# A streaming encoder step on one core: own values in one full-shape product, spatial products joined, one unread product more at the start, the last norm by logarithm and exponential

## The chip, the cores and the metric

The kernel runs on one core of a Trainium2 chip. The metric is the device time of one execution in microseconds (us); lower is better. TensorE multiplies (PE, with its weight loads in a queue called PEld), VectorE (DVE), ScalarE (ACT) and GpSimd (POOL) work on tiles of 128 partitions, and transfers are issued from the queues of SP, ACT and POOL.

## The reference

Two layers and a final norm run over 256 prompt rows and 8 x 16 sample rows, 384 rows in all, with a model width of 2048. Layer 0 is two kinds of attention side by side; layer 1 is a gated MLP with a spatial mix. Cut to the parts that the change touches:

```python
# layer 0, samples: cached and new keys and values are joined, per head
go = fox_core(gq, k_all, v_all, ...)      # softmax weights @ (128 cached + 16 new) values
to = sb_core(tq, sk_all, sv_all, ...)     # stick-breaking weights @ the same
# layer 1: 16 groups of 256 columns, one lower-triangular 128x128 matrix each
w = jnp.where(causal, w_sp[:, :L, :L], 0.0)
mixed = jnp.einsum('gts,bnsgc->bntgc', w, vg) + b_sp   # prompt: 128-row chunks; samples: 16 rows each
h = h + einsum('bsn,nd->bsd', u * mixed * silu(z), w_out1)
# the end
y = h * rsqrt(mean(h * h, -1) + 1e-6) * final_g
```

## The kernel before

All 384 rows are one batch of three blocks of 128 rows (tb = 0 and 1 the prompt, tb = 2 the eight samples). The large products keep fp32 precision by splitting both operands into a high and a low part: `products` (lines 100 to 102) issues three products of 128x512 for each block of rows and each 128 rows of a weight matrix. The weights come by SP (`wload`), ACT makes the high part (line 84), DVE the low part (line 86). Everything else is fitted in between these dense products.

The order on each engine is fixed when the program is built: the framework puts ready instructions into the queues by a model of their times, so a step can stand far ahead of the code next to it. An engine then takes its queue strictly in that order.

**Attention.** Heads are worked in 8 pairs (`quad` has four heads, `attended` finishes a pair). In `head`, the samples' weights against the 16 new keys of each sample stand as a 128x32 block, which DVE turns in 32x32 blocks into `own` (line 718). The samples' output `od` is summed in PSUM from four 32x32 products with `own` (line 728), one for each group of two samples, and eight products with the cached values (line 732; 128 rows by 32 columns of the array). The prompt's output is three full 128x128 products (lines 734 to 736). These products are in plain fp32, and the trace shows each as two records. PT, the turned weights that lines 732 to 736 need, come back from DRAM through POOL's queue and a DVE transpose (line 721).

**Spatial mix.** For each of eight chunks c of 512 columns, three blocks tb and two groups i, lines 932 to 934 issue three products of 256 columns into half a PSUM bank, and line 937 adds the bias and multiplies by the gate.

**Start.** `keep_warm` issues products of ones that nobody reads. The first block of x is turned on TensorE (line 248), three transposes, the third of rows that another transfer brings.

**End.** `last` makes the last four of 32 weight blocks for each block of rows in five pieces; DVE adds the piece to h1 (line 994), ACT sums squares (line 996), DVE multiplies by the gain (line 998). `norm` then has DVE prepare the mean (lines 1002 to 1004), POOL take the power -0.5 (line 1005), and ACT and DVE scale the rows (lines 1012, 1015) and send them out. `norm(0)` and `norm(1)` stand ahead of the last block's pieces, `norm(2)` ends the program.

Of the kernel before, what the change touches and what calls it, by code (L numbers as in the profile page):

```python
# [8 lines left out]
F32 = mybir.dt.float32  # L9
F32R = mybir.dt.float32r  # L10
AF = mybir.ActivationFunctionType
# [4 lines left out]
P = 128  # L16
# [21 lines left out]
def tile_hybrid_step(  # L38
# [20 lines left out]
    def nm(s):  # L59
        n_names[0] += 1  # L60
        return f"{s}_{n_names[0]}"
# [100 lines left out]
    with ExitStack() as l0:  # L162
# [76 lines left out]
        def x_blocks(k):  # L239
            b = lp.tile([P, 2 * T], F32, tag="PT", name=nm("xT"))  # L240
            then("DVE", lambda: V.transpose(out=b, in_=xblk[k]))
            xblk[k], xblk[k + 1] = b[:, :T], b[:, T:]

        def x_transposes(k):
            if k < FB:
                b = bank()
                for tb in range(NT):
                    then("PE", lambda: PE.transpose(b[:, tb * P:(tb + 1) * P], xs[k // 4][:, tb, k % 4 * P:k % 4 * P + P], ident))
            else:
                b = xblk[k]  # L250
# [89 lines left out]
        with late():  # L340
            V.tensor_reduce(out=par[:, 4:5], in_=par[:, :4], axis=AX.X, op=ALU.add)
            V.tensor_scalar(out=slotb[:, 0:1], in0=par[:, 4:5], scalar1=-1.0, scalar2=-NEG, op0=ALU.add, op1=ALU.mult)
            V.tensor_scalar(out=slotb[:, 1:2], in0=par[:, 4:5], scalar1=NEG, scalar2=None, op0=ALU.mult)
        masks = []
        for strict in (0, 1):
# [6 lines left out]
            for s in range(2):  # L352
                with late():
                    V.tensor_scalar(out=md[:, s * P:(s + 1) * P], in0=md[:, s * P:(s + 1) * P], scalar1=slotb[:, s:s + 1], scalar2=None, op0=ALU.add)
            new = lp.tile([P, 2 * T], F32, tag="PT", name=nm("new"))[:, :P]
            V.memset(new, 0.0)
# [29 lines left out]
        def forget(o):  # L386
# [39 lines left out]
            gains(1)  # L426
            nFT = lp.tile([8, 2 * T], F32, tag="PT", name="nFT")[:, :T]
            V.tensor_scalar(out=nFT, in0=FT, scalar1=-1.0, scalar2=None, op0=ALU.mult)
# [219 lines left out]
        def head(g, h, kT, values, qT, kc, vc, gate):  # L648
            fox = g < 2
            mp, md = masks[0 if fox else 1]  # L650
            if fox:

                fb = lp.tile([P, 2, T], F32, tag="fb", name=nm("fb"))
                fc = lp.tile([P, P], F32, tag="fc", bufs=1, name=nm("fc"))
                G.dma_start(fb[:, 0, :2 * P], nFd[h, :2 * P].partition_broadcast(P))
                G.dma_start(fb[:, 0, 2 * P:], nFd[h, :P].partition_broadcast(P))
                G.dma_start(fb[:, 1, 2 * P:TW], nFd[h, 2 * P:].rearrange("(j k) -> j k", k=32).unsqueeze(1).broadcast_to([4, 32, 32]))
                G.dma_start(fc, nFcd[:, h, :].unsqueeze(1).broadcast_to([8, 16, P]))
                G.tensor_tensor(out=fb[:, 0, :], in0=fb[:, 0, :], in1=mp, op=ALU.add)
                G.tensor_tensor(out=fb[:, 1, 2 * P:TW], in0=fb[:, 1, 2 * P:TW], in1=md[:, 2 * P:], op=ALU.add)  # L660
                G.tensor_tensor(out=fb[:, 1, :2 * P].rearrange("p (s k) -> p s k", s=2), in0=md[:, :2 * P].rearrange("p (s k) -> p s k", s=2),
                                in1=fc.unsqueeze(1).broadcast_to([P, 2, P]), op=ALU.add)
                mp, md = fb[:, 0, :], fb[:, 1, :TW]

# [51 lines left out]

            own = lp.tile([P, 32], F32, tag="own", bufs=4, name=nm("own"))
            V.transpose(out=own, in_=weights[:, 5 * P:])
            blk = yield
            PT = lp.tile([P, 2 * T], F32, tag="PT", name=nm("PT"))[:, :5 * P]  # L720
            yield V.transpose(out=PT, in_=blk)
# [3 lines left out]
            od, ot = ob[:, 2 * P:3 * P], ob[:, :2 * P]  # L725
            for j in range(4):
                js = slice(32 * j, 32 * j + 32)
                PE.matmul(od[js, :], lhsT=own[js, :], rhs=vn[js, 2, :], start=True, stop=False)
            for s in range(2):
                for j in range(4):  # L730
                    js = slice(32 * j, 32 * j + 32)
                    PE.matmul(od[js, :], lhsT=PD[:, s * P + 32 * j:s * P + 32 * j + 32], rhs=vc[:, 2 * j + s, :], start=False, stop=(s == 1))
            yield
            PE.matmul(ot[:, :P], lhsT=PT[:, 2 * P:T], rhs=vn[:, 0, :], start=True, stop=True)
            PE.matmul(ot[:, P:2 * P], lhsT=PT[:, :P], rhs=vn[:, 0, :], start=True, stop=False)
# [76 lines left out]
    with ExitStack() as l1:  # L812
# [91 lines left out]
        for c in range(8):  # L904
# [10 lines left out]
            else:  # L915
# [7 lines left out]
                for j, ck in enumerate(order[:3]):  # L923
                    aside[ck] = x[:, j, :]
                    G.dma_start(x[:, j, :], wlast(*ck))
            for tb in range(NT):
                m = bank()
                for i in range(2):
                    cs = slice(i * 256, i * 256 + 256)
                    (wh, wl), (vh, vl) = wTs[i], vhl  # L930
                    o = m[:, cs]
                    PE.matmul(o, lhsT=wh[:, tb // 2, :], rhs=vh[:, tb, cs], start=True, stop=False)
                    PE.matmul(o, lhsT=wh[:, tb // 2, :], rhs=vl[:, tb, cs], start=False, stop=False)
                    PE.matmul(o, lhsT=wl[:, tb // 2, :], rhs=vh[:, tb, cs], start=False, stop=True)
                for i in range(2):
                    gh = gate[:, tb, i * 256:(i + 1) * 256]
                    V.scalar_tensor_tensor(out=gh, in0=m[:, i * 256:(i + 1) * 256], scalar=bcol[:, tb // 2, 2 * c + i:2 * c + i + 1], in1=gh, op0=ALU.add, op1=ALU.mult)
            gT = lp.tile([P, NT * 4, P], F32, tag="gTt", bufs=1, name=nm("gTt"))
# [61 lines left out]
        def norm(tb):  # L1000
            r0, r1 = rst2[:, tb, 0:1], rst2[:, tb, 1:2]
            V.tensor_reduce(out=r0, in_=ssq2[:, tb, :4], axis=AX.X, op=ALU.add)
            V.tensor_scalar(out=r0, in0=r0, scalar1=1.0 / DM, scalar2=RMS_EPS, op0=ALU.mult, op1=ALU.add)
            V.scalar_tensor_tensor(out=r0, in0=ssq2[:, tb, 4:5], scalar=1.0 / DM, in1=r0, op0=ALU.mult, op1=ALU.add)  # L1004
            G.tensor_tensor(out=r1, in0=r0, in1=ex[:, 0:1], op=ALU.pow)  # L1005
            ht = h1[3][:, tb, 256:]
# [54 lines left out]
```

## Time and profile before

| | us |
|---|---|
| median of 3 runs (1795.68 to 1795.89) | 1795.76 |
| the profiled execution, its own time | 1797.74 |
| span of the profile | 1796.0 |
| PE busy (share of the span) | 1785.7 (99%) |
| DVE / ACT / POOL busy | 941.9 / 725.3 / 389.5 |

The span covers the first to the last record of the profiled execution, and its own time lies 1.74 us above it. A matmul's duration in a row is longer than its share of the engine, since products overlap in the array: what one costs is the distance between starts in a dense row of them.

### The profile page before, as it was taken

What the parts mean: (1) busy time and instruction counts of PE and PEld (TensorE: products, weight loads), DVE (VectorE), ACT (ScalarE), POOL (GpSimd) and SP (SyncE); (2) the same over time, 40 slices, a digit from 0 to 9 for tenths busy, and PEclk for the clock granted to TensorE, in tenths of its full rate; (3) what the DMA queues carried; (4) which work ended last, traced back from release to release, by engine and by line L of the source; (5) the groups of instructions that cost most, each with busy time, mean ns of one, the idle gap of its engine ahead of it and who ended that gap; (6) DMA issues with size and microseconds to landing.
All of it is one profiled execution on the core that took longest, in us unless ns stands there. A gap on an engine that the chain in (4) does not pass through costs nothing. (4 is left out here: it accounts for less than half of the span.)

```text
span 1796.0 us, 24812 instructions
## 1 busy us (share of the span) xinstructions
PE 1785.7 (99%) x8707; PEld 1477.4 (82%) x8707; DVE 941.9 (52%) x1600; ACT 725.3 (40%) x1301; POOL 389.5 (22%) x584
## 2 busy tenths in 40 slices
PE   9999999999999999999999999999999999999998
PEld 8987788888888788888888888888888888888887
DVE  6337465457448455534434546455555464455366
ACT  5435354346337244433333433433333333433344
POOL 6526543223311211200300121220120210220020
PEclk9999999999999999999999999999999999999999
DMA  7968988768767777644544454455444554455553
GB/s 215 228 187 207 270 219 226 221 176 227 216 188 192 225 199 192 193 136 129 137 129 123 139 159 127 147 148 145 146 147 119 154 154 129 147 144 153 155 146 119
DMA packets 184749, 305.97 MB, mean 170 GB/s; under 512 B 23512, under 2 KB 61968, under 8 KB 184624
## 3 DMA queue, kind: packets, MB, share of 16 engines
q1 hardware_dynamic: 127696, 225.37, 42.9%
q0 software_dynamic: 26096, 62.89, 14.0%
q10 hardware_dynamic: 30832, 16.13, 3.0%
q8 instruction: 68, 1.11, 0.3%
q14 instruction: 57, 0.47, 0.1%
HBM read 268.57 MB, written 29.42 MB: 166 GB/s over the span
## 5 line engine op out<-in xcount | busy, mean ns | idle before, releaser
L86 DVE TENSOR_TENSOR wlo<-raw,whi 128x512 fp32r<-128x512 f32 x784 | 536.7, 693 | 723.8 <-ACT whi L84 722.7
L101 PE MATMUL d<-wlo,slot 128*128 128x512 f32 x2349 | 911.9, 389 | 0.1
L102 PE MATMUL d<-whi,slot 128*128 128x512 f32 x2349 | 911.2, 389 | 0.0
L84 ACT ACTIVATE whi<-raw 128x512 fp32r<-128x512 f32 x784 | 493.2, 631 | 903.0 <-PE d L102 847.2
L100 PE MATMUL d<-whi,slot 128*128 128x512 f32 x2349 | 822.9, 390 | 0.0
L100 PEld LDWEIGHTS d<-whi,slot 128*128 128x128 f32 x2349 | 440.4, 188 | 94.8 <-issue 2.4
L101 PEld LDWEIGHTS d<-wlo,slot 128*128 128x128 f32 x2349 | 441.1, 188 | 91.5 <-DVE wlo L86 1.0
L102 PEld LDWEIGHTS d<-whi,slot 128*128 128x128 f32 x2349 | 441.1, 188 | 90.8
L128 POOL DMA_DIRECT2D gTt<-trn x128 | 77.9, 617 | 312.8 <-issue 159.0
L439 POOL DMA_DIRECT2D slot<-d x48 | 44.0, 923 | 133.3 <-DVE wlo L86 54.3
L884 POOL DMA_DIRECT2D wr<-in_w_sp_dram x64 | 34.9, 552 | 113.0 <-DVE wT L888 99.5
L539 POOL DMA_DIRECT2D slot<-wd x32 | 27.1, 855 | 95.0 <-DMA wd<-pr 39.3
L877 DVE TENSOR_TENSOR slot<-d,slot 128x512 f32<-128x512 f32 x48 | 32.4, 688 | 13.8 <-PE d L102 13.8
L833 POOL DMA_DIRECT2D slot<-in_sgu_ln_g_dram x8 | 4.5, 568 | 135.0 <-PE d L102 135.0
L500 POOL DMA_DIRECT2D kcache<-in_cache_sb_k_dram x32 | 24.9, 785 | 32.1 <-DVE KT L668 32.1
L500 POOL DMA_DIRECT2D kcache<-in_cache_fox_k_dram x32 | 25.0, 788 | 24.8 <-DVE KT L668 23.9
L759 POOL DMA_DIRECT2D blk<-h1d x12 | 10.9, 919 | 72.2 <-DMA h1d<-slot 34.6
L849 POOL DMA_DIRECT2D bcol<-in_b_sp_dram x1 | 1.2, 1176 | 116.1 <-DVE w L848 116.1
L827 POOL TENSOR_SCALAR rsv<-mvr 128x3 f32<-128x3 f32 x1 | 0.5, 538 | 108.1 <-DVE mvr L826 108.1
L824 DVE BATCH_NORM_STATS2 stats<-vt 128x6 f32<-128x512 f32 x24 | 16.2, 689 | 11.6 <-ACT vt L823 11.6
L912 DVE SCALAR_TENSOR_TENSOR gate<-d,rstd,gate 128x512 f32<-128x512 f32 x24 | 17.4, 748 | 7.3 <-PE d L102 7.3
L909 ACT ACTIVATE gate<-d,rstd 128x512 f32<-128x512 f32 x24 | 16.5, 690 | 11.2 <-PE d L102 11.1
(256 smaller groups left out, 1287.5 us busy)
## 6 DMA issues: line engine op xcount, KB each, us to landing
raw<-in_w_in_dram SPq DMA_DIRECT2D x640, 256.0 KB, 2.9
raw<-in_w_out_dram SPq DMA_DIRECT2D x189, 256.0 KB, 3.4
slot<-d POOLq DMA_DIRECT2D x48, 192.0 KB, 6.3
d<-slot ACTq DMA_DIRECT2D x24, 256.0 KB, 4.0
gTt<-trn POOLq DMA_DIRECT2D x128, 48.0 KB, 3.5
wd<-pr ACTq DMA_DIRECT2D x16, 320.0 KB, 5.6
slot<-wd POOLq DMA_DIRECT2D x32, 160.0 KB, 5.1
kcache<-in_cache_fox_k_dram POOLq DMA_DIRECT2D x32, 128.0 KB, 5.5
```

The source lines that it names most:

```text
L84: highs.append(S.activation(hi, raw, AF.Copy).ins)
L86: splits.append(V.tensor_tensor(out=lo, in0=raw, in1=f32(hi), op=ALU.subtract).ins)
L100: PE.matmul(o, lhsT=his[k][:, t], rhs=hi[:, 0, :], start=(k == first), stop=False)
L101: PE.matmul(o, lhsT=his[k][:, t], rhs=lo[:, 0, :], start=False, stop=False)
L102: mm = PE.matmul(o, lhsT=los[k][:, t], rhs=hi[:, 0, :], start=False, stop=(k == last))
L128: G.dma_start(dst[32 * j:32 * j + 32, :, 32 * a:32 * a + 32], trn[32 * a:32 * a + 32, :, 32 * j:32 * j + 32])
L439: r = G.dma_start(blk[32 * j:32 * j + 32].rearrange("p h (a d) -> p (h a) d", d=32), d[:, :, 32 * j:32 * j + 32].rearrange("h (a p) d -> p ...
L500: G.dma_start(k[32 * j:32 * j + 32].rearrange("p (b d) -> p b d", d=32), (c_fox_k, c_sb_k)[n // 8][:, :, n % 8, 32 * j:32 * j + 32].rearra ...
L539: G.dma_start(blk[32 * j:32 * j + 32].rearrange("p j (a d) -> p (j a) d", d=32), wd[:, :, :, 32 * j:32 * j + 32].rearrange("j x (a p) d -> ...
L877: evicted = V.tensor_tensor(out=h1[c][:, tb, :], in0=o[tb], in1=h1[c][:, tb, :], op=ALU.add)
L884: G.dma_start(wr[js, 0, :].rearrange("p (a s) -> p a s", s=32), w_sp[g, :, js].rearrange("(a p) s -> p a s", p=32))
L912: V.scalar_tensor_tensor(out=gate[:, tb, :], in0=o[tb], scalar=rstd[:, tb:tb + 1], in1=gate[:, tb, :], op0=ALU.mult, op1=ALU.mult)
```

## The change

Four edits. (1) `own` is laid out on the diagonal of a 128x128 tile by a POOL multiplication with a mask `diag`, so that the samples' new values take one full product in place of four 32x32 ones, and it is issued behind the cached values instead of ahead of them. (2) The spatial products of a group take both prompt blocks at once (512 columns), the samples' block stays at 256. (3) One unread product of ones stands between the second and third transpose of the first block. (4) `norm` takes the power by ACT: a logarithm, with the mean's last part as scale and bias, and an exponential. Beside these, some tiles change size or tag (`xT` is turned in two halves in other buffers, `PT`, `fb`).

```diff
         def x_blocks(k):
-            b = lp.tile([P, 2 * T], F32, tag="PT", name=nm("xT"))
-            then("DVE", lambda: V.transpose(out=b, in_=xblk[k]))
-            xblk[k], xblk[k + 1] = b[:, :T], b[:, T:]
+            both = xblk[k]
+            for kk in range(2):
+                xblk[k + kk] = b = lp.tile([P, 512], F32, tag="KT", bufs=4, name=nm("xT"))[:, :T]
+                then("DVE", lambda: V.transpose(out=b, in_=both[:, kk * T:kk * T + T]))
...
                 for tb in range(NT):
+                    if k == 0 and tb == 2:
+
+                        keep_warm(1)
                     then("PE", lambda: PE.transpose(b[:, tb * P:(tb + 1) * P], xs[k // 4][:, tb, k % 4 * P:k % 4 * P + P], ident))
...
+        diag = lc.tile([P, 4], F32, name="diag")
+        V.memset(diag, 1.0)
+        select(diag, [[-32, 4]], 0, 1)
+        select(diag, [[32, 4]], 31, -1)
...
-            own = lp.tile([P, 32], F32, tag="own", bufs=4, name=nm("own"))
-            V.transpose(out=own, in_=weights[:, 5 * P:])
+            turned = lp.tile([P, 32], F32, tag="ownT", name=nm("ownT"))
+            V.transpose(out=turned, in_=weights[:, 5 * P:])
+            own = lp.tile([P, P], F32, tag="own", bufs=4, name=nm("own"))
+            G.tensor_tensor(out=own.rearrange("p (j q) -> p j q", j=4), in0=turned.unsqueeze(1).broadcast_to([P, 4, 32]),
+                            in1=diag.unsqueeze(2).broadcast_to([P, 4, 32]), op=ALU.mult)
...
-            for j in range(4):
-                js = slice(32 * j, 32 * j + 32)
-                PE.matmul(od[js, :], lhsT=own[js, :], rhs=vn[js, 2, :], start=True, stop=False)
             for s in range(2):
                 for j in range(4):
                     js = slice(32 * j, 32 * j + 32)
-                    PE.matmul(od[js, :], lhsT=PD[:, s * P + 32 * j:s * P + 32 * j + 32], rhs=vc[:, 2 * j + s, :], start=False, stop=(s == 1))
+                    PE.matmul(od[js, :], lhsT=PD[:, s * P + 32 * j:s * P + 32 * j + 32], rhs=vc[:, 2 * j + s, :], start=(s == 0), stop=False)
             yield
+            PE.matmul(od, lhsT=own, rhs=vn[:, 2, :], start=False, stop=True)
...
-            for tb in range(NT):
-                m = bank()
-                for i in range(2):
-                    cs = slice(i * 256, i * 256 + 256)
-                    (wh, wl), (vh, vl) = wTs[i], vhl
-                    o = m[:, cs]
-                    PE.matmul(o, lhsT=wh[:, tb // 2, :], rhs=vh[:, tb, cs], start=True, stop=False)
...
+            for i in range(2):
+                cs = slice(i * 256, i * 256 + 256)
+                (wh, wl), (vh, vl) = wTs[i], vhl
+
+                for j, tbs in ((0, slice(0, 2)), (1, slice(2, 3))):
+                    n = tbs.stop - tbs.start
+                    m = bank()[:, :n * 256].rearrange("p (t c) -> p t c", t=n)
+                    PE.matmul(m, lhsT=wh[:, j, :], rhs=vh[:, tbs, cs], start=True, stop=False)
...
             V.tensor_scalar(out=r0, in0=r0, scalar1=1.0 / DM, scalar2=RMS_EPS, op0=ALU.mult, op1=ALU.add)
-            V.scalar_tensor_tensor(out=r0, in0=ssq2[:, tb, 4:5], scalar=1.0 / DM, in1=r0, op0=ALU.mult, op1=ALU.add)
-            G.tensor_tensor(out=r1, in0=r0, in1=ex[:, 0:1], op=ALU.pow)
+
+            S.activation(r1, ssq2[:, tb, 4:5], AF.Ln, scale=1.0 / DM, bias=r0)
+            S.activation(r1, r1, AF.Exp, scale=-0.5)
```

How the queues change. TensorE's queue in the second pair of heads, before (a is a PSUM bank of the small products, d one of the dense ones); first where the products with `own` stood, then, 61 rows later, where the rest of the pair stood:

```order
L102 MATMUL d_1752<-whi_2123,slot_136 128x512
L728 MATMUL a_2227<-vnat_647,own_1843 32x128
L100 MATMUL d_2160<-whi_2165,slot_129 128x512
L728 MATMUL a_2227<-vnat_647,own_1843 32x128 x2
L101 MATMUL d_2160<-wlo_2167,slot_129 128x512
L102 MATMUL d_2160<-whi_2165,slot_130 128x512
L100 MATMUL d_2160<-whi_2171,slot_129 128x512
L101 MATMUL d_2160<-wlo_2173,slot_129 128x512
L102 MATMUL d_2160<-whi_2171,slot_130 128x512
L728 MATMUL a_2227<-vnat_647,own_1843 32x128
L100 MATMUL d_2161<-whi_2165,slot_129 128x512
```

```order
L102 MATMUL d_2161<-whi_2314,slot_132 128x512
L732 MATMUL a_2240<-vcache_2083,PT_2223 32x128 x3
L732 MATMUL a_2227<-vcache_2081,PT_2225 32x128 x8
L732 MATMUL a_2240<-vcache_2083,PT_2223 32x128 x5
L734 MATMUL a_2227<-vnat_647,PT_2225 128x128
L735 MATMUL a_2227<-vnat_647,PT_2225 128x128
L736 MATMUL a_2227<-vnat_647,PT_2225 128x128
L734 MATMUL a_2240<-vnat_647,PT_2223 128x128
```

The same pair now, whole:

```order
L102 MATMUL d_2174<-whi_2344,slot_134 128x512
L741 MATMUL a_2239<-vcache_2093,PT_2237 32x128 x8
L741 MATMUL a_2248<-vcache_2095,PT_2235 32x128 x8
L743 MATMUL a_2239<-vnat_657,own_1859 128x128
L744 MATMUL a_2239<-vnat_657,PT_2237 128x128
L745 MATMUL a_2239<-vnat_657,PT_2237 128x128
L746 MATMUL a_2239<-vnat_657,PT_2237 128x128
L743 MATMUL a_2248<-vnat_657,own_1888 128x128
L744 MATMUL a_2248<-vnat_657,PT_2235 128x128
L745 MATMUL a_2248<-vnat_657,PT_2235 128x128
L746 MATMUL a_2248<-vnat_657,PT_2235 128x128
L100 MATMUL d_2174<-whi_2350,slot_133 128x512
```

The products with `own` have left the dense stretch and stand among the full ones. Four of the eight pairs now read like this. In the first pair the cached products of the second head stand behind the first head's full products. In three pairs part of the cached products has moved ahead, as here in the first pair of the third quad:

```order
L741 MATMUL a_4599<-vcache_3426,PT_4597 32x128 x4
L100 MATMUL d_4564<-whi_4567,slot_129 128x512
L101 MATMUL d_4564<-wlo_4569,slot_129 128x512
L102 MATMUL d_4564<-whi_4567,slot_130 128x512
L100 MATMUL d_4564<-whi_4573,slot_129 128x512
L101 MATMUL d_4564<-wlo_4575,slot_129 128x512
L102 MATMUL d_4564<-whi_4573,slot_130 128x512
L741 MATMUL a_4599<-vcache_3426,PT_4597 32x128 x4
L741 MATMUL a_4608<-vcache_3428,PT_4595 32x128 x8
```

ACT's queue at the end of the program, before (sq: the sums of squares of the last block; the slots are h1):

```order
L996 ACTIVATE sq_3237_15974,ssq_15709<-slot_5878 128x256
L996 ACTIVATE sq_3239_15991,ssq_15709<-slot_5878 128x256
L1012 ACTIVATE slot_5875<-slot_5875,rst_15710 128x512
L1012 ACTIVATE slot_5877<-slot_5877,rst_15710 128x256
L1013 DMA out_dram<-slot_5875 128x512
```

and now:

```order
L1006 ACTIVATE sq_3264_15912,ssq_15647<-slot_5884 128x256
L1006 ACTIVATE sq_3266_15929,ssq_15647<-slot_5884 128x256
L1015 ACT_TABLE_LOAD
L1015 ACTIVATE rst_15648<-ssq_15647,rst_15648 128x1
L1016 ACT_TABLE_LOAD
L1016 ACTIVATE rst_15648<-rst_15648 128x1
L1023 ACTIVATE slot_5881<-slot_5881,rst_15648 128x512
L1023 ACTIVATE slot_5883<-slot_5883,rst_15648 128x256
L1024 DMA out_dram<-slot_5881 128x512
```

Two loads of a function table have come in with the logarithm and the exponential; the same four rows stand in `norm(0)` and `norm(1)`, ahead of the last block's squares.

## Rows read from the trace of the kernel before

**Rows 1.** The page, part 1: busy time, share of the span, instructions.

```profile
PE 1785.7 (99%) x8707; PEld 1477.4 (82%) x8707; DVE 941.9 (52%) x1600; ACT 725.3 (40%) x1301; POOL 389.5 (22%) x584
```

**Rows 2.** PE's waits: who, for whom, us in total, times, longest.

```profile
PE a L933 <- DVE vl L91: 0.6, 3, 0.2
```

**Rows 3.** Timeline of PE, first pair: start, us, line, out<-in, records.

```profile
178.09 0.39 PE L102 MATMUL d<-whi,slot 128*128 128x512 f32 x1
178.41 0.42 PE L728 MATMUL a<-vnat,own 32*32 32x128 f32 x8
...
180.59 0.39 PE L735 MATMUL a<-vnat,PT 128*128 128x128 f32 x2
...
181.48 0.39 PE L736 MATMUL a<-vnat,PT 128*128 128x128 f32 x2
...
181.94 0.40 PE L101 MATMUL d<-wlo,slot 128*128 128x512 f32 x1
```

**Rows 4.** Timeline of PE, second pair, whose own products came earlier.

```profile
207.08 0.39 PE L102 MATMUL d<-whi,slot 128*128 128x512 f32 x1
207.40 1.10 PE L732 MATMUL a<-vcache,PT 128*32 128x128 f32 x32
...
210.11 0.39 PE L102 MATMUL d<-whi,slot 128*128 128x512 f32 x1
```

**Rows 5.** Timeline of PE, one own product (two records) among dense ones.

```profile
192.10 0.39 PE L102 MATMUL d<-whi,slot 128*128 128x512 f32 x1
192.42 0.40 PE L728 MATMUL a<-vnat,own 32*32 32x128 f32 x2
...
193.09 0.40 PE L101 MATMUL d<-wlo,slot 128*128 128x512 f32 x1
```

**Rows 6.** The tiles own and fb: ns min/median/max, first and last start.

```profile
L718 DVE STREAM_TRANSPOSE own<-pr x16: 191/197/206, 145.1 to 576.8; 128x32 f32<-128x32 f32 x16
...
L661 POOL TENSOR_TENSOR fb<-md,fc x8: 727/752/1132, 90.9 to 277.7; 128x256 f32<-128x256 f32 x8
```

**Rows 7.** Timeline of PE: nine spatial products in a row; 30 dense ones.

```profile
1001.01 0.28 PE L934 MATMUL a<-vh,wTl 128*128 128x256 f32 x1
...
1001.97 0.28 PE L934 MATMUL a<-vh,wTl 128*128 128x256 f32 x1
...
1777.83 0.39 PE L990 MATMUL d<-wlast,slot 128*128 128x512 f32 x1
...
1784.41 0.39 PE L992 MATMUL d<-wlast,slot 128*128 128x512 f32 x1
```

**Rows 8.** Timeline of ACT at the end; in brackets the idle time ahead.

```profile
1777.27 1.12 ACT L1012 ACTIVATE slot<-slot,rst 128x512 f32<-128x512 f32 x2 [1.00 <-POOL rst L1005]
...
1782.93 0.63 ACT L996 ACTIVATE sq<-slot 128x512 f32<-128x512 f32 x1 [1.42 <-DVE slot L994]
...
1785.62 0.63 ACT L996 ACTIVATE sq<-slot 128x512 f32<-128x512 f32 x1 [1.97 <-DVE slot L994]
...
1788.24 0.42 ACT L996 ACTIVATE sq<-slot 128x256 f32<-128x256 f32 x1 [0.95 <-DVE rst L1003]
1788.57 0.19 ACT L996 ACTIVATION_READ_ACCUMULATOR sq<-slot 128x1 f32 x1
1789.72 1.12 ACT L1012 ACTIVATE slot<-slot,rst 128x512 f32<-128x512 f32 x2 [0.97 <-POOL rst L1005]
```

**Rows 9.** Timeline of ACT around the one table load inside the kernel.

```profile
1014.82 1.28 ACT L909 ACT_TABLE_LOAD   x1
1016.12 0.69 ACT L909 ACTIVATE gate<-d,rstd 128x512 f32<-128x512 f32 x1
```

**Rows 10.** Timeline of PE and its weight loads in the first 11 us.

```profile
5.01 0.18 PEld L248 LDWEIGHTS a<-ident,slot 128*128 128x128 f32 x1 [0.54 <-DMA slot<-in_x_sample_dram]
...
8.21 1.63 PE L282 MATMUL d<-whi,slot 128*128 128x512 f32 x3
9.63 1.07 PE L282 MATMUL d<-wlo,slot 128*128 128x512 f32 x3
```

More of the change, by code (lines that the diff above doesn't have):

```diff
@@ L354, in tile_hybrid_step @@
                     V.tensor_scalar(out=md[:, s * P:(s + 1) * P], in0=md[:, s * P:(s + 1) * P], scalar1=slotb[:, s:s + 1], scalar2=None, op0=ALU.add)
-            new = lp.tile([P, 2 * T], F32, tag="PT", name=nm("new"))[:, :P]
+            new = lp.tile([P, 5 * P], F32, tag="PT", name=nm("new"))[:, :P]
             V.memset(new, 0.0)
@@ L426, in forget @@
             gains(1)
-            nFT = lp.tile([8, 2 * T], F32, tag="PT", name="nFT")[:, :T]
+            nFT = lp.tile([8, 5 * P], F32, tag="PT", name="nFT")[:, :T]
             V.tensor_scalar(out=nFT, in0=FT, scalar1=-1.0, scalar2=None, op0=ALU.mult)
@@ L651, in head @@
             if fox:
-                fb = lp.tile([P, 2, T], F32, tag="fb", name=nm("fb"))
+                fb = lp.tile([P, T + TW], F32, tag="fb", name=nm("fb"))
                 fc = lp.tile([P, P], F32, tag="fc", bufs=1, name=nm("fc"))
-                G.dma_start(fb[:, 0, :2 * P], nFd[h, :2 * P].partition_broadcast(P))
-                G.dma_start(fb[:, 0, 2 * P:], nFd[h, :P].partition_broadcast(P))
-                G.dma_start(fb[:, 1, 2 * P:TW], nFd[h, 2 * P:].rearrange("(j k) -> j k", k=32).unsqueeze(1).broadcast_to([4, 32, 32]))
+                G.dma_start(fb[:, :2 * P], nFd[h, :2 * P].partition_broadcast(P))
+                G.dma_start(fb[:, 2 * P:T], nFd[h, :P].partition_broadcast(P))
+                G.dma_start(fb[:, T + 2 * P:], nFd[h, 2 * P:].rearrange("(j k) -> j k", k=32).unsqueeze(1).broadcast_to([4, 32, 32]))
                 G.dma_start(fc, nFcd[:, h, :].unsqueeze(1).broadcast_to([8, 16, P]))
-                G.tensor_tensor(out=fb[:, 0, :], in0=fb[:, 0, :], in1=mp, op=ALU.add)
-                G.tensor_tensor(out=fb[:, 1, 2 * P:TW], in0=fb[:, 1, 2 * P:TW], in1=md[:, 2 * P:], op=ALU.add)
-                G.tensor_tensor(out=fb[:, 1, :2 * P].rearrange("p (s k) -> p s k", s=2), in0=md[:, :2 * P].rearrange("p (s k) -> p s k", s=2),
+                G.tensor_tensor(out=fb[:, :T], in0=fb[:, :T], in1=mp, op=ALU.add)
+                G.tensor_tensor(out=fb[:, T + 2 * P:], in0=fb[:, T + 2 * P:], in1=md[:, 2 * P:], op=ALU.add)
+                G.tensor_tensor(out=fb[:, T:T + 2 * P].rearrange("p (s k) -> p s k", s=2), in0=md[:, :2 * P].rearrange("p (s k) -> p s k", s=2),
                                 in1=fc.unsqueeze(1).broadcast_to([P, 2, P]), op=ALU.add)
-                mp, md = fb[:, 0, :], fb[:, 1, :TW]
+                mp, md = fb[:, :T], fb[:, T:]
             KTt = []
@@ L715, in head @@
             nc.scalar.dma_start(wd.rearrange("x q k -> q x k"), weights[:, :5 * P].rearrange("q (x k) -> q x k", k=P))
-            own = lp.tile([P, 32], F32, tag="own", bufs=4, name=nm("own"))
-            V.transpose(out=own, in_=weights[:, 5 * P:])
+            turned = lp.tile([P, 32], F32, tag="ownT", name=nm("ownT"))
[3 more added lines that the diff above has]
+                            in1=diag.unsqueeze(2).broadcast_to([P, 4, 32]), op=ALU.mult)
             blk = yield
-            PT = lp.tile([P, 2 * T], F32, tag="PT", name=nm("PT"))[:, :5 * P]
+            PT = lp.tile([P, 5 * P], F32, tag="PT", name=nm("PT"))
             yield V.transpose(out=PT, in_=blk)
@@ L925, in tile_hybrid_step @@
                     G.dma_start(x[:, j, :], wlast(*ck))
-            for tb in range(NT):
-                m = bank()
-                for i in range(2):
-                    cs = slice(i * 256, i * 256 + 256)
-                    (wh, wl), (vh, vl) = wTs[i], vhl
-                    o = m[:, cs]
-                    PE.matmul(o, lhsT=wh[:, tb // 2, :], rhs=vh[:, tb, cs], start=True, stop=False)
[L933 to L937, printed above, removed]
+            for i in range(2):
[5 more added lines that the diff above has]
+                    PE.matmul(m, lhsT=wh[:, j, :], rhs=vh[:, tbs, cs], start=True, stop=False)
+                    PE.matmul(m, lhsT=wh[:, j, :], rhs=vl[:, tbs, cs], start=False, stop=False)
+                    PE.matmul(m, lhsT=wl[:, j, :], rhs=vh[:, tbs, cs], start=False, stop=True)
+                    gh = gate[:, tbs, cs]
+                    V.scalar_tensor_tensor(out=gh, in0=m, scalar=bcol[:, j, 2 * c + i:2 * c + i + 1], in1=gh, op0=ALU.add, op1=ALU.mult)
             gT = lp.tile([P, NT * 4, P], F32, tag="gTt", bufs=1, name=nm("gTt"))
```

## The prediction

> **What bounds the kernel now.** I read the page's busy line first: PE is busy for 1785.7 of 1796.0 us [rows 1]. Such a share can hide stalls, so the list of PE's waits comes next. Behind the first microsecond it has one entry, 0.6 us in all for the low part of the spatial values [rows 2]. So TensorE is the bound from the first product to the last, and everything ahead of the end costs exactly what it takes in TensorE's queue. What an operation takes there is read from distances between starts, not from durations: 30 dense products start in 6.58 us, 0.227 each, though each row says 0.39 [rows 7]. Only behind the last product does another chain set the end: square, mean, power, scaling, store [rows 8].
>
> So the change is worth (a) what it saves in TensorE's queue, less (b) what it adds to the chain behind the last product, with (c) the first ten microseconds apart.
>
> **Own values.** The reader should see that the four 32x32 products hardly cost their work; they cost the change of shape. One of them (two records) stands among dense products [rows 5]: from 192.10 to 193.09 are 0.99 us, in which two dense products need 0.45. The interruption costs 0.54. A whole group of four alone costs 0.56, so the shape change is nearly all. The order of before has seven such interruptions: two next to each other (1.07 together), this one (0.54), one group of four (0.56), and one stray product in each of three later pairs (0.54 each): 3.79 in all.
>
> The pairs themselves: the first takes 181.94 - 178.09 less two dense products, 3.85 - 0.45 = 3.40 [rows 3]. Seven of the eight read so, within 0.02, also where one own product had gone ahead. The second pair, whose own products all had gone ahead, takes 210.11 - 207.08 - 0.45 = 2.58 [rows 4]. Before: 7 x 3.39 + 2.58 + 3.79 = 30.1 us.
>
> The second pair [rows 4] is what four of the new pairs are, plus two full products. A full fp32 product of this size costs (181.48 - 180.59) / 4 = 0.22 [rows 3]. So those four pairs take 2.58 + 0.45 = 3.03 each, 12.1. In the first pair the cached products stand in two places between full ones, one more change there and back, about 0.1 each way (178.41 - 178.09 less 0.227 is 0.09 [rows 3]): 3.23. In three pairs part of the cached products stands ahead of six or twelve dense ones. That interruption costs 0.54 like any other, but takes along about half of a group of eight, whose 16 records take 0.51 here (32 records in 1.03): +0.27, so 3.30 each, 9.9. After: 25.2. **Saved: 4.9 us.** Bounds: if each moved part costs a full interruption on top and the first pair two more, 3.7; if the moves cost nothing, 5.6.
>
> What feeds them is hidden. POOL's new multiplication is not in the trace; the nearest row, 128x256, takes 0.75 [rows 6], and this has half the elements, so 0.4 to 0.8, sixteen times, on an engine that is busy for 22% [rows 1]. The first `own` is turned at 145.1 [rows 6] and first used at 178.4 [rows 3], now later. POOL's reads of the turned weights queue behind it, but they wait for those weights' write anyway. Without that cover a pair would be 0.8 late.
>
> **Spatial products.** Nine products of 256 columns start within 0.96 us, 0.120 each; two of them against one of 512 is 0.240 against 0.227 [rows 7]. 48 pairs are joined: 0.6 us saved. The waits of 0.6 us [rows 2] may go, since the low part now comes later in the queue in those chunks, or stay as a wait for the samples' high part. Taken: **0.9 saved**, bounds 0.6 and 1.3. DVE's four gate multiplications instead of six are beside the bound.
>
> **The end.** A table load takes 1.28 us, and the next function starts 1.30 behind the load's start [rows 9]. The two functions on 128x1 are not in the trace; the nearest row, reading out the accumulator on 128x1, takes 0.19 [rows 8]. So a norm adds 2 x 1.28 + 2 x 0.2 = 2.97 us to ACT's own queue, in front of the scaling. In the last norm the square starts at 1788.24, its sum is read until 1788.76 and the scaling starts at 1789.72, 0.96 later [rows 8]. Now 2.97: +2.0.
>
> The first two norms stand ahead of the last block's squares in the same queue. Each swaps a wait of 1.0 for POOL [rows 8] against 2.97: ACT runs 3.9 us late. It had idle time there, 1.42, 1.97 and 0.95 [rows 8], but these were waits for PE's pieces, and once it is late the squares alternate with DVE's additions and gain products, 0.6 us each way. Walked step by step in the new order, the second square of the last block comes 3.4 us late and the last one 2.4. Bounds: 0 and 3.9. DVE waits with ACT, and the additions behind it hold PSUM banks, but four banks of pieces lie between PE and DVE, so PE doesn't wait. **Lost: 2.0 + 2.4 = 4.4 us,** bounds 2.0 and 5.9.
>
> The Trainium skill (ScalarE: Activation LUTs, What ACT_TABLE_LOAD costs) gives 1283 ns for the load and some 1380 ns of draining besides, 2.66 us for a switch. By [rows 9] nothing of that kind stands behind the load, and it followed the activation before it at once. By the page's 2.66 the sum would come out 7 us slower than before, not 1.3 faster. The same page (Table sets) says that a logarithm and an exponential share one set and need one load; the order of this program has two for each norm, so that rule gives nothing here, and with one load the sum would be about 1791.
>
> **The start.** The unread product fills a wait: the third transpose waits 0.54 us for the samples' rows [rows 10], and the product takes about 0.45 there (0.22 [rows 3], at half the clock). Its own cost is 0 to 0.2; I take 0.1. In the rows the clock is at its lower level here: the three products from 8.21 take 1.42 us until the next three, 0.47 each against 0.227 later, and by the 1.07 of the latter the level rises at about 10.1 [rows 10]. If the filled gap lets it rise earlier, say 1.7 us behind the gap near 6.7, up to half of 3.4 us comes back; ACT and DVE, through which the next transposed block goes, leave some 1.3. Nothing in the trace says that this gap holds the level down. The turned halves of x and the masks change only DVE and POOL, which PE doesn't wait for.
>
> **Sum.** -4.9 - 0.9 + 4.4 + 0.1 = -1.3. The profiled execution took 1797.74 (span 1796.0), so the same execution would be at 1796.4; the median of the runs is 1795.76, 2.0 below it, and from there the forecast is 1794.4.
>
> **Rivals.**
> *The clock rises earlier.* The gap is the last larger one before 6.7, which speaks for it; that the clock stayed low for another 3.4 us of nearly dense work speaks against. Another -1.3: 1793.1. With the savings at their upper bounds (another -1.1) it is about 1792.
>
> *The table loads cost more than their rows.* If each of these six switches holds ACT for as long again as its load, 2.57 instead of 1.28, the backlog grows without being caught up: the same walk gives an end 12.1 us later in place of 4.4, so 1794.4 + 7.7 = 1802.1, slower than before. Each microsecond more on a load costs six at the end, so the sum turns against the change from 1.5 us a load on. The rows [rows 9] speak against it: the function ran at once behind the load. For it speaks only that these rows are a single load, and that two in a row with a 128x1 function between them stand nowhere in the trace. By the Trainium skill's 2.66 (ScalarE: Activation LUTs, What ACT_TABLE_LOAD costs) it would be 1802.7.
>
> *The shapes change as often as before.* If the full product with `own`, which adds into a bank that four column strips have just written, has to wait for them, or the moved cached products cost like the strays, the pairs stay near 30: then the end's 4.4 stands against 0.9, 1794.4 + 4.9 = 1799.3 at worst; with half of it, 1796.9. The second pair [rows 4] speaks against, since the three prompt products follow the cached ones into the same bank at 0.22.
>
> **How the numbers follow.** Chances: forecast 58%, earlier clock 27%, shapes 10%, loads 5%. The measurement of this kernel tells about 0.2% from no change, 3.6 us. Faster by that (below 1792.2) takes the earlier clock with savings near their bounds, or an ACT backlog that vanishes: 13%. Slower (above 1799.4) takes the loads, or the shapes at their worst: 6%. The rest, 81%, is within. The range must reach over the earlier clock below and the shapes' half above: 1791.8 to 1797.4.
>
> **What would show it.** In the trace after: pairs of heads near 3.0 to 3.3 us between dense products, with no 32x32 record left; chunks of the spatial mix about 0.1 us shorter; six table loads of 1.28, the last scaling 4 to 5 us later behind the last product than now; the start's products at 0.227 from about 10.1 on. PE's waits stay under 2 us. Wrong it would be if PE waits for `own` or PT, if PE's span before the last product shrinks by clearly less than 5 or more than 7 us, or if the end takes other than 2 to 6 us more.

## The result, and the profile after

The changed kernel takes 1799.42 us (median of 12 runs, 1797.75 to 1801.78) against 1795.90 us of the kernel before on the same chip (12 runs, 1795.67 to 1797.55): a ratio of 1.0019, interval 1.0011 to 1.0027. It is 3.5 us slower, where the forecast had it 1.3 us faster, and its runs spread twice as widely. The profiled execution took 1800.07 us, its span is 1798.4.

The page's busy line and the whole list of PE's waits after the change, to be read against [rows 1, 2]:

```profile
PE 1781.0 (99%) x8565; PEld 1475.6 (82%) x8565; DVE 941.9 (52%) x1584; ACT 734.3 (41%) x1313; POOL 393.6 (22%) x599
```

```profile
PE d L100 <- ACT whi L84: 2.2, 1, 2.2
PE a L219 <- DVE ones L134: 1.1, 1, 1.1
PE d L101 <- DVE wlo L86: 0.2, 1, 0.2
```

PE is busy 4.7 us less, as hoped, and yet the span is longer. The list has a new first entry: one wait of 2.2 us for the high part of dense weights, which [rows 2] do not have. First the parts that went as forecast.

**Own values.** Timeline of PE, the second pair of heads, to be read against [rows 3, 4]:

```profile
207.55 0.39 PE L102 MATMUL d<-whi,slot 128*128 128x512 f32 x1
207.87 1.08 PE L741 MATMUL a<-vcache,PT 128*32 128x128 f32 x32
208.88 0.49 PE L743 MATMUL a<-vnat,own 128*128 128x128 f32 x2
...
210.69 0.48 PE L100 MATMUL d<-whi,slot 128*128 128x512 f32 x1
211.01 0.39 PE L101 MATMUL d<-wlo,slot 128*128 128x512 f32 x1
```

From 207.55 to 211.01, less two dense products, are 3.01 us for a pair with its new values (forecast 3.03). Over all eight pairs and what is left of stray parts it is 25.6 us where the kernel before has 30.2: 4.6 saved (forecast 4.9). POOL's diagonal multiplication takes 0.40 at the median, sixteen times, and nobody waits for it.

**The start.** Timeline of PE, against [rows 10]:

```profile
4.67 0.63 PE L219 MATMUL a<-ones 128*128 128x128 f32 x2
...
7.34 0.94 PE L286 MATMUL d<-whi,slot 128*128 128x512 f32 x3
8.12 0.85 PE L286 MATMUL d<-wlo,slot 128*128 128x512 f32 x3
8.81 0.39 PE L100 MATMUL d<-whi,slot 128*128 128x512 f32 x1
```

The three products from 7.34 now take 0.78 to the next three, 0.26 each, so they run at the upper level (2.4 GHz), which before was reached at about 10.1, some 3 us later. The first product of L100 starts at 8.81, 1.7 us earlier than in the profiled execution before. That is the first rival, as far as the two traces go.

**The end.** Timeline of ACT behind the last sum of squares, against [rows 8]:

```profile
1788.36 0.42 ACT L1006 ACTIVATE sq<-slot 128x256 f32<-128x256 f32 x1 [1.01 <-DVE rst L1013]
1788.68 0.19 ACT L1006 ACTIVATION_READ_ACCUMULATOR sq<-slot 128x1 f32 x1
1788.89 1.28 ACT L1015 ACT_TABLE_LOAD   x1
1790.18 0.29 ACT L1015 ACTIVATE rst<-ssq,rst 128x1 f32<-128x1 f32 x1
1790.49 1.28 ACT L1016 ACT_TABLE_LOAD   x1
1791.79 0.20 ACT L1016 ACTIVATE rst<-rst 128x1 f32<-128x1 f32 x1
1792.02 1.12 ACT L1023 ACTIVATE slot<-slot,rst 128x512 f32<-128x512 f32 x2
```

From the read-out's end (1788.87) to the scaling are 3.15 us, where it was 0.96: 2.2 more. The loads cost what [rows 9] say, and two in a row no more. PE's last product starts at 1784.54 here and at 1787.38 before; from it to the last scaling are 7.48 us against 2.34, so the end costs 5.1 (forecast 4.4).

**Where the rest went.** With 1.7 us from the start, 4.7 from the own values and something from the spatial products, PE's last product should stand at least 6.4 us earlier. It stands 2.84 earlier. The starts of the dense products, paired off in order, show where: the lead grows to 6.0 us by 664 us, where the products of layer 0's output weights run, and is 1.9 at 690. (The texts written ahead of the first runs below say 6.6; their argument hangs on the loss, which is the same.) Four microseconds went in one place. PE's timeline there, and then the window behind the gap (busy us and instructions of PE, PEld, DVE, ACT and POOL; the last three numbers are the granted clock, the DMA share and GB/s):

```profile
679.39 0.39 PE L102 MATMUL d<-whi,slot 128*128 128x512 f32 x1
682.00 1.64 PE L100 MATMUL d<-whi,slot 128*128 128x512 f32 x3 [2.22 <-ACT whi L84]
683.43 0.63 PE L101 MATMUL d<-wlo,slot 128*128 128x512 f32 x1
...
685.52 0.40 PE L100 MATMUL d<-whi,slot 128*128 128x512 f32 x1
```

```profile
682.00:686.00 4.00, 4.00 (x11) 3.18 (x12) 2.56 (x5) 1.51 (x3) 0.00 (x0) 0.57 0.47 133
```

2.6 us lie between two starts, and then the products stand 0.43 apart until 685.5: the granted clock of 682 to 686 is 0.57, so most of that stretch is at 1.2 GHz. Wait and slow products together are the 4 us. The chain of work that ended last says what was late:

```profile
666.35 11.11 DMA blk<-h1d
677.48 1.79 DVE vnat L775
679.94 0.97 DVE slot L787 x2
682.00 1.64 PE d L100 x3
```

That is the hand-over between the layers. The result of layer 0 is written to `h1d` and read back in 32x32 blocks (`h1_turn`, L769), DVE turns the block (L775), and ACT and DVE split it (L786, L787). These splits stand in ACT's queue ahead of the next high parts L84. The second block's transfer takes 11.11 us; DVE waits 4.18 for it, ACT 6.72, PE 2.2. Before, DVE turned this block at 679.42 without waiting for the transfer, and PE, 6.0 us less advanced, never noticed. DVE's turn of the second block, before and after:

```profile
679.42 1.77 DVE L765 STREAM_TRANSPOSE vnat<-blk 128x1536 f32<-128x1536 f32 x1
```

```profile
677.48 1.78 DVE L775 STREAM_TRANSPOSE vnat<-blk 128x1536 f32<-128x1536 f32 x1 [4.18 <-DMA blk<-h1d]
```

Nothing in the diff touches that transfer. But its landings are slower, and so are those of other transfers into layer 0's own buffers. The median from issue to landing of the four parts of a block is 6.9 us before (longest 8.0) and 8.7 after (longest 11.1); of the K caches' pieces 5.5 and 6.8, of the V caches' only 7.0 and 7.3. The windows of the kernel before (first) and after:

```profile
20.00:200.00 180.00, 180.00 (x1071) 151.93 (x1069) 95.10 (x196) 83.75 (x173) 90.85 (x132) 1.00 0.79 209
200.00:400.00 200.00, 200.00 (x1094) 162.94 (x1087) 108.41 (x188) 82.85 (x154) 70.24 (x88) 1.00 0.81 218
```

```profile
20.00:200.00 180.00, 180.00 (x1051) 153.57 (x1050) 95.42 (x196) 83.55 (x172) 91.82 (x128) 1.00 0.85 211
200.00:400.00 200.00, 200.00 (x1070) 164.03 (x1069) 112.19 (x194) 85.90 (x160) 68.47 (x89) 1.00 0.85 218
```

The same bytes per second, but the DMA engines are busy for 0.85 instead of 0.79 to 0.81. In layer 1 (0.49 to 0.50 in both) nothing differs. What sets layer 0 apart stands in the built program's table of addresses: the new tile `diag`, 16 bytes in a partition, is allocated ahead of layer 0's pool, addresses go in steps of 32, and so every large buffer behind it begins 32 bytes past a multiple of 256.

```
first byte    before   after    diag of 256 B   diag of 64 B
kcache        153088   153120   153344          153152
vcache        161280   161312   161536          161344
kT and blk    205312   204320   204544          204352
modulo 256         0       32        0               64
```

### The profile page after: what moved, and what is told of

Read it like the earlier page. It is cut to its first block, busy times and chain, and to the rows that moved or that the text cites. A ratio compares the mean times of both kernels' runs of the same rounds, so it can differ in the third digit from the quotient of the medians.

```text
span 1798.4 us, 24560 instructions
## 1 busy us (share of the span) xinstructions
PE 1781.0 (99%) x8565; PEld 1475.6 (82%) x8565; DVE 941.9 (52%) x1584; ACT 734.3 (41%) x1313; POOL 393.6 (22%) x599
## 4 chain that ended last, share of the span: by engine, by line
PE 60%; DMA 1%; ACT 1%; DVE 1%; POOL 0%; issue 0%; DVEq 0%; ACTq 0%
PE d L100 19%; PE d L101 19%; PE d L102 19%; DMA blk<-h1d 1%; PE d L1001 0%; PE d L1000 0%; PE d L1002 0%; PE a L943 0%; PE a L944 0%; PE a L945 0%; ACT L1016 0%; ACT L1015 0%; DVE vnat L775 0%; ACT sq L1006 0%; DVE slot L1008 0%; DVE slot L787 0%
## 5 line engine op out<-in xcount | busy, mean ns | idle before, releaser
L86 DVE TENSOR_TENSOR wlo<-raw,whi 128x512 fp32r<-128x512 f32 x784 | 539.0, 697 | 719.0 <-ACT whi L84 718.0
L84 ACT ACTIVATE whi<-raw 128x512 fp32r<-128x512 f32 x784 | 492.6, 631 | 885.6 <-PE d L102 830.4
L100 PE MATMUL d<-whi,slot 128*128 128x512 f32 x2349 | 824.2, 391 | 2.2 <-ACT whi L84 2.2
L100 PEld LDWEIGHTS d<-whi,slot 128*128 128x128 f32 x2349 | 441.3, 188 | 97.9 <-ACT whi L84 3.5
L769 POOL DMA_DIRECT2D blk<-h1d x12 | 11.0, 920 | 74.2 <-DMA h1d<-slot 60.9
L677 DVE STREAM_TRANSPOSE KT<-kcache 128x512 f32<-128x512 f32 x32 | 19.8, 675 | 8.0 <-DMA kcache<-in_cache_fox_k_dram 4.5
L91 DVE TENSOR_TENSOR wlo<-raw,whi 128x512 fp32r<-128x512 f32 x16 | 11.0, 690 | 22.0 <-ACT whi L90 22.0
```

Source lines behind the costliest of these rows:

```text
L84: highs.append(S.activation(hi, raw, AF.Copy).ins)
L86: splits.append(V.tensor_tensor(out=lo, in0=raw, in1=f32(hi), op=ALU.subtract).ins)
L100: PE.matmul(o, lhsT=his[k][:, t], rhs=hi[:, 0, :], start=(k == first), stop=False)
L677: V.transpose(out=t, in_=kc[:, hf * 4 * P:(hf + 1) * 4 * P])
```

## The experiments

**Theory A, addresses:** transfers into buffers that start off a multiple of 256 bytes take longer, and at the layers' border that is what PE waits for. **Theory B, margin:** PE came 6.0 us too early for a transfer that could not be earlier. A different order of the instructions, the third candidate, is ruled out: the built programs of kernel 1 and the changed kernel, and those of kernel 2 and the kernel before, have the same instructions in the same order in every queue, and differ in addresses (and the row length of `diag`) alone. The first four kernels ran on one chip, beside 1795.45 us of the kernel before.

**1. `diag` on 256 bytes, all else as changed.**

```diff
-        diag = lc.tile([P, 4], F32, name="diag")
+        diag = lc.tile([P, 64], F32, name="diag")[:, :4]
```

> The changed kernel with one figure other: the 16-byte tile diag takes 256 bytes, so that every buffer of layer 0 behind it starts on a multiple of 256 bytes again, as in the kernel before. Theory A (addresses): the lost 4 us between the two layers (a wait of 2.2 us for split weights and a stretch at half clock behind it) come from slower transfers into buffers that start 32 bytes off. Then the DMA share of 20 to 400 us falls from 0.85 to about 0.79 to 0.81, the re-read blocks of h1d land in some 7 us instead of 8.7, TensorE does not wait near 680 us, and the time is about 1795.5 us (4 less), with less spread from run to run. Theory B (margin): the products reach the layer's end 6.6 us earlier than before and overtake the re-read whatever its address; then the wait near 680 us stays at 1.5 us or more and the time stays at 1798 to 1800 us.

Measured: 1796.25 us (1794.93 to 1796.61), ratio 1.0000 (0.9991 to 1.0009). The window of 20 to 200 us, PE's waits and the landings of `blk` (200 to 400: a share of 0.81):

```profile
20.00:200.00 180.00, 180.00 (x1051) 153.60 (x1050) 95.47 (x196) 83.98 (x171) 91.39 (x127) 1.00 0.79 210
```

```profile
PE a L219 <- DVE ones L134: 1.1, 1, 1.1
PE d L286 <- DVE slot L261: 0.4, 1, 0.4
PE d L101 <- DVE wlo L86: 0.2, 1, 0.2
```

```profile
DMA to landing us min/median/max: 3.9/7.2/8.9
```

The share is that of before, the wait is gone, 3.2 us came back (2.7 if each kernel is taken against the kernel before on its own chip), and the runs lie within 1.7 us instead of 4. So PE's lead is not too much for the transfer: theory B falls.

**2. The kernel before, with an unread tile of 16 bytes in the same place.**

```diff
+        off = lc.tile([P, 4], F32, name="off")
         masks = []
```

> The kernel before with an unread 16-byte tile at the place of diag: nothing else is changed, and every buffer of layer 0 starts 32 bytes past a multiple of 256. Theory A: the DMA share of 20 to 400 us rises from 0.80 to about 0.84, the K cache lands in about 6.7 us instead of 5.5 and the blocks of h1d in 8 to 9 instead of 6.9. The time rises by 0 to 2 us, since this kernel reaches the layer's end 6.6 us later and its second block was turned without waiting for its transfer. Theory B: shares, landings and time are those of the kernel before, 1795.9 us.

Measured: 1801.37 us (1800.34 to 1803.73), ratio 1.0033 (1.0020 to 1.0046). The same window (200 to 400: 0.84), the first of PE's waits, DVE's turns of the first two blocks:

```profile
20.00:200.00 180.00, 179.44 (x1060) 151.38 (x1059) 93.05 (x195) 82.92 (x171) 89.10 (x129) 1.00 0.83 206
```

```profile
PE d L100 <- ACT whi L84: 2.4, 2, 1.9
```

```profile
667.80 1.78 DVE L766 STREAM_TRANSPOSE vnat<-blk 128x1536 f32<-128x1536 f32 x1 [2.66 <-DMA blk<-h1d]
...
686.51 1.78 DVE L766 STREAM_TRANSPOSE vnat<-blk 128x1536 f32<-128x1536 f32 x1 [2.03 <-DMA blk<-h1d]
```

An allocation that nothing reads or writes makes the kernel 5.9 us slower. The mechanism is that of theory A; its size was mis-set (0 to 2 expected), since without any lead of PE the border already lacks that much room. The starts of the dense products say where, in the two profiled executions, which are 5.3 apart: 1.1 us are lost by 98 us, 1.3 between 420 and 570, and at the border 0.9 at 672 behind the first block and 2.4 at 691 behind the second; 0.4 comes back in layer 1.

**3. Power as before, `diag` on 16 bytes.** The diff undoes the last edit of the change alone (L1015 and L1016 become the multiply-add on DVE and the power on POOL of the kernel before).

> The changed kernel with the last norm's power on GpSimd as before (no logarithm, no exponential, no table load at the end); diag stays at 16 bytes. Theory of the sum: the end gives back all of its 5.1 us (2.2 in the last norm, the rest in the backlog that the first two norms leave on ScalarE), so about 1794.4 us with the wait between the layers still there. Rival: only the last norm counts, 2.2 us, about 1797.2 us.

Measured: 1795.32 us (1792.31 to 1798.42), 4.1 under the changed kernel, with the wait near 680 (2.6 us) still there. The end costs more than its last norm's 2.2.

**4. Both: power as before, `diag` on 256 bytes.**

> Both: diag on 256 bytes and the last norm by power as before. If addresses (4 us) and end (5.1 us) add up, about 1790.4 us, clearly faster than both kernels: the three edits on TensorE's queue and at the start are then worth their 5.5 us. Theory B with the end: 1794.5. If only the last norm's own 2.2 us came back: 1793.3.

Measured: 1790.68 us (1790.03 to 1791.58), ratio 0.9973 (0.9962 to 0.9984), as the sum had it. The two costs add up, and what is left of the change is a gain of 4.8 us. The next kernels build on this one.

**5. `diag` on 64 bytes.** (Kernel 4 with `[P, 16]` in place of `[P, 64]`; kernels 5, 7, 8 and 9 ran beside 1796.20 of the kernel before.)

> The kernel that ran at 1790.68 us (diag on 256 bytes, power in the last norm) with diag on 64 bytes: the buffers of layer 0 start 64 bytes past a multiple of 256, instead of on one or 32 past. It asks which boundary counts. Theory 256: transfers are as slow as with 32 (DMA share of 20 to 400 us near 0.84, h1d blocks in 8 us or more), the wait near 680 us is back, and the time is about 1795. Theory 64 (or anything at or below it): share 0.80, no wait, 1790.7 us. By the section on how a descriptor splits into AXI transactions of the Trainium skill's DMA: Bandwidth & Descriptors, which has starts on 256 bytes, it would be the first.

Measured: 1793.96 us (1790.44 to 1796.5). The window and the first of the waits that concern the border (200 to 400: 0.84):

```profile
20.00:200.00 180.00, 180.00 (x1051) 153.63 (x1050) 96.12 (x198) 84.40 (x174) 91.52 (x129) 1.00 0.85 211
```

```profile
PE d L100 <- ACT whi L84: 1.0, 1, 1.0
```

The transfers are as slow as with 32 bytes, so a multiple of 64 does not do; 256 does, and 128 was not tried. The Trainium skill (DMA: Bandwidth & Descriptors, How a descriptor splits into AXI transactions) says that a transaction must start on a multiple of 256 bytes, so that a descriptor which starts elsewhere also fetches bytes ahead of its start, which cost beats. It says so of what is read, while here the address that is written to moved. The shares of 0.85 agree with a rule of this kind; that this split is the cause, no run here shows.

**6. 32 bytes ahead of the re-read block alone.** Kernel 4 with one more unread tile: the caches of K and V stay on multiples of 256; the buffer of `blk` and those behind it move. (With kernels 10 and 11 below beside 1796.78 of the kernel before.)

```diff
             FT = lp.tile([8, 2 * T], F32, tag="pr", name="FT")[:, :T]
+            lp.tile([P, 8], F32, tag="gap", bufs=1, name="gap")
```

> The same with 32 bytes ahead of the buffer that takes the re-read blocks of h1d: it and what lies behind it (transposed queries, the bias tiles) start 32 bytes past a multiple of 256, while the caches of K and V and the tiles that feed the other transfers stay on it. Theory: the late block is enough, since the wait near 680 us is for it alone: landings of 8 us or more there, a wait of about 2 us, 1793 to 1795 us. Rival: it takes the load that all transfers of layer 0 lay on the engines, the K and V caches above all: no wait, 1790.7 us.

Measured: 1793.92 us (1791.96 to 1795.98), 2.8 over the same kernel without the gap (1791.15). The window, the wait and the landings of `blk`:

```profile
20.00:200.00 180.00, 180.00 (x1051) 153.58 (x1050) 96.07 (x195) 83.85 (x172) 92.67 (x129) 1.00 0.81 211
```

```profile
PE d L100 <- ACT whi L84: 1.8, 1, 1.8
```

```profile
DMA to landing us min/median/max: 6.2/8.2/10.1
```

With the engines' load in the attention stage near that of before, the wait is back. Of the buffers that moved, `blk` alone takes transfers at the border, so the slower re-read is enough by itself, and the address that a transfer writes to is what counts there. The way to PE is longer here than in the changed kernel, though: DVE's turn of the first block, and the last high part of ACT ahead of the second:

```profile
659.54 1.78 DVE L776 STREAM_TRANSPOSE vnat<-blk 128x1536 f32<-128x1536 f32 x1 [2.17 <-DMA blk<-h1d]
```

```profile
677.00 0.63 ACT L84 ACTIVATE whi<-raw 128x512 fp32r<-128x512 f32 x1 [3.85 <-DMA raw<-in_w_out_dram]
```

DVE waits for the first block, and SP for the low parts behind it (up to 7.0 us, in kernel 4's second trace 4.9), which free the buffers of the weights. The weights' transfers then start late and take up to 10.9 us to land (7.6 there), though their own buffers are on multiples of 256, and the second block is not waited for at all. In kernel 5 it is the same (waits of 1.2 for the first block, 3.1 for weights, 0.2 for the second block).

**7. Logarithm and exponential in the last norm alone.** (`diag` on 256 bytes; power if `tb < 2`.)

> The changed kernel with diag on 256 bytes (1796.25 us), logarithm and exponential in the norm of the last 128 rows alone, and power for the first two blocks. If the end's 5.1 us are 2.2 for the last norm and the rest the backlog of the first two on ScalarE, this gives 1790.7 + 2.2 = 1792.9 us. Rival: the last norm's two loads cost all of it, and the first two lie under products: 1795.5 to 1796.3.

Measured: 1793.24 us (1792.17 to 1794.32), ratio 0.9982 (0.9973 to 0.9991). From the last product to the last scaling are 4.5 us, 2.2 over the 2.34 of before. So of the end's 5.1 us 2.2 are the last norm and 2.9 the backlog of the first two.

**8. One table for both functions, loaded ahead of the end.** (`diag` on 256 bytes.)

```diff
+        with tc.issue_after(highs[-1]):
+            S.preload_act_table_set("natural_log_exp_and_others")
         with tc.issue_after(evicted.ins):
             while order:
                 last_split()
```

> The changed kernel with diag on 256 bytes and one table that has both functions, loaded once after the last Silu behind the last split of layer 1's weights; the three norms then hold no table load. If the loads are the cost of the end (6 of 1.28 us), the last norm's way from the fourth square's read-out to the scalings takes about 0.6 us instead of 3.15 (power: 0.96) and the time is 1790.2 to 1790.7 us. Rival: that the norms stand on ScalarE's queue costs by itself, since the squares of the last block queue behind them; then it stays above 1791.5.

Measured: 1790.36 us (1789.99 to 1790.7), ratio 0.9968 (0.9955 to 0.9980). Timeline of ACT at the end:

```profile
1781.21 0.19 ACT L1008 ACTIVATION_READ_ACCUMULATOR sq<-slot 128x1 f32 x1
1781.43 0.29 ACT L1017 ACTIVATE rst<-ssq,rst 128x1 f32<-128x1 f32 x1
1781.75 0.20 ACT L1018 ACTIVATE rst<-rst 128x1 f32<-128x1 f32 x1
1781.99 1.12 ACT L1025 ACTIVATE slot<-slot,rst 128x512 f32<-128x512 f32 x2
```

From the read-out's end to the scaling are 0.6 us. The whole cost of the end was the loads; the functions on ACT are as good as the power on POOL, and no better in the total.

**9. Without the unread product** (kernel 4 without `keep_warm(1)`).

> The same kernel without the unread product among the first transposes. By the two profiled executions, in which the first dense product stands at 10.5 us before and at 8.8 us after, the edit is worth 1.7 us: 1792.4 us here. Rival: the profiled execution of the kernel before was 2 us above its median, and most of its executions had the early clock already; then the median stays at 1790.7 to 1791 and only some runs are 1.7 us longer.

Measured: 1790.33 us (1789.61 to 1791.09), ratio 0.9967 (0.9955 to 0.9980), against 0.9973 and 0.9967 of kernel 4 with it. It is worth nothing that shows. Timeline of PE at the start:

```profile
4.19 0.97 PE L249 MATMUL a<-ident,slot 128*128 128x128 f32 x3
...
5.97 1.49 PE L283 MATMUL d<-whi,slot 128*128 128x512 f32 x3
...
7.54 0.95 PE L283 MATMUL d<-whi,slot 128*128 128x512 f32 x3
```

Here the transposes hardly wait for the samples' rows (0.2 us), and the clock is up by 7.5 us without the extra product. In the two other traces without the product (that of before, [rows 10], and kernel 2), which have a wait of 0.5 us, it rose at about 10.1. The first product of L100 starts at 10.5 and 10.6 us in those two, at 9.0 here, and at 8.5 to 9.2 in every trace with the product. The profiled execution of before was 2.0 us over its median; that most executions have no such wait would explain both, but it is argued. Nor do five runs exclude a gain in some executions: of the 23 runs of the kernel before beside kernels 6, 10 and 11, 11 lie at 1797.2 us or above and 12 at 1796.8 or below.

**10 and 11. Parts taken back:** the own values as before, the spatial products as before, each in kernel 4, and kernel 4 once more beside them.

> The kernel of 1790.68 us once more (diag on 256 bytes, power in the last norm), so that the next three are compared on one chip: 1790.3 to 1791 us, 4.8 to 5.5 us under the kernel before.

> The same with the new values' product as in the kernel before: four products on 32 rows each for a head, opened first, and the transposed weights without the diagonal form. By the cost of its records in the two traces (30.2 us in eight pairs of heads before, 25.6 after) it is worth 4.7 us: 1795.4 us. If part of it was hidden or lies in the spread: 1794 or less.

> The same with the spatial product as in the kernel before (three products of 256 columns for each block of rows). The forecast had 0.9 us for it; the records of the two traces have 19.7 us in eight blocks before and 18.1 after, 1.5 less, but the weights of the joined product wait 1.5 us in all for ScalarE's split. 1791.6 by the first, 1792.2 by the second; no change if the wait takes it.

Measured: 1791.15 us for kernel 4 (1790.33 to 1791.27), 1795.68 without the own edit (1794.85 to 1796.53), 1791.55 without the spatial edit (1790.88 to 1791.96). The own edit is worth 4.5 us, the spatial one 0.4, which is as small as the spread.

## Why the prediction was wrong

**The step that failed** is the first: "TensorE is the bound from the first product to the last, and everything ahead of the end costs exactly what it takes in TensorE's queue". It held for the kernel before, and for kernels 1, 4, 8 and 9. It failed where the border between the layers had less room than the slower transfers took: "PE's waits stay under 2 us" was broken at 682 us (2.22), and PE's span before the last product shrank by 2.8 us, under the 5 that the prediction named as a sign of being wrong. The step behind it is that I costed tiles by what is computed in them. The masks "change only DVE and POOL, which PE doesn't wait for"; that a new tile moves every later one, and that a transfer's time hangs on its address, was in no term, bound or rival. Its size is 3.2 us (kernel 1) to 4.6 (kernel 4 against 3). That the transfers had little room at the border could have been read in the trace of the kernel before, in a window that the prediction does not read:

```profile
656.00:664.00 8.00, 8.00 (x37) 6.64 (x36) 5.59 (x8) 3.85 (x9) 0.39 (x1) 1.00 1.03 254
```

The DMA engines' share is 1.03 there. Such a share says where to look, not that a wait follows: kernel 4's second trace has 0.97 from 650 to 656 and 0.98 from 664 to 672, and no wait.

**The rest of the sum,** without that, was 2 us too hopeful: kernel 1, the change without the shift, is at 1796.25, inside the range, but 0.8 above the kernel before beside it where 1.3 below was forecast.

- Own values: 4.9 forecast, 4.6 in the records, 4.5 by the run. The shape argument of [rows 3, 4, 5] holds, and the rival that the shapes change as often falls.
- Spatial products: 0.9 forecast, 0.4 measured, under its lower bound of 0.6 and as small as the spread. The weight loads of the joined products now wait for ACT's split of the values, 1.5 us in three places.
- Start: 0.1 lost by forecast, nothing measured. The rival of the earlier clock came true in the trace and not in the median. The trace of before was an execution above its median, which the sum noted and then did not use to doubt the rows of the start.
- End: 4.4 forecast, 5.1 in the trace (2.2 for the last norm where 2.0 stood, 2.9 of backlog where 2.4 stood). The rival of dearer loads falls: each takes 1.28, two in a row too. The Trainium skill's 2.66 us for a switch (ScalarE: Activation LUTs, What ACT_TABLE_LOAD costs) is not seen here: the logarithm starts 1.29 behind the start of its load. That one set holds both functions (the same page, Table sets) is shown by kernel 8, where one load by the set's name sufficed for all three norms; the prediction had said what that would be worth, 1791.

With these sizes, -4.5 - 0.4 + 5.1 + 3.2 to 4.6 is 3.4 to 4.8 us slower; 3.5 was measured. (The 5.1 is from the traces; kernels 1 and 4, which differ in the end alone, are 5.6 apart, and the sum is then 3.9 to 5.3.)

## What to carry to other kernels

A small tile allocated ahead of large ones moves them all: keep what transfers write to on multiples of 256 bytes (32 and 64 off were slow here, 128 was not tried), or look at the table of addresses before a change's time is read as that of its instructions. Where a queue is said to be the bound, look for the places where its feeders arrive last, above all borders between stages where the DMA engines' share is near 1. A table load at a program's end costs as often as it stands in the queue; load one set that has all the functions, by name, where its engine is idle.

## What was not expected of the hardware

Layer 0's buffers 32 or 64 bytes off a multiple of 256 raise the busy share of the DMA engines from 0.79 and 0.81 to 0.83 to 0.85 at the same rate, and the re-read block's landings from 7 to some 8 to 9 us. An unused tile of 16 bytes cost 5.9 us of 1796. And a wait of PE can cost more than itself: after 2.6 us in which nothing started, the products came at half rate for another 3.5 us. It need not: after its wait of 1.9 us kernel 2 has a granted clock of 1.00 from 691 to 694 us, while kernel 6, after a wait of 1.8, has 0.53 from 684 to 687.
